# Gate and up products by a seven-product scheme over half of the k-tiles, with weight splits of 2048 elements

## The chip, the core and the metric

The kernel runs on one core of a Trainium2 chip. The metric is the device time of one execution in microseconds (us): 2843.92 us as the median of 3 runs (2843.08 to 2844.45).

## What is computed

Two decoder layers over 256 tokens of width 2048, all in f32: layer 0 mixes with latent attention (MLA), layer 1 with a gated delta rule (GDN). Each layer then has a SwiGLU feed-forward network (FFN) and a gated per-layer embedding (PLE).

```python
h = h + mixer(rms_norm(h, mixer_norm[i]), ...)
gate, up = jnp.split(rms_norm(h, ffn_norm[i]) @ w_gate_up[i], 2, axis=-1)   # 2048 x 11264
h = h + (jax.nn.silu(gate) * up) @ w_down[i]                                # 5632 x 2048
h = h + per_layer_embedding(h, p[i], ...)
```

## The kernel before

Every product with weights goes through `linear` (L216). The 256 tokens are two tiles of 128 (`T` = 2). An f32 operand is split in two fp32r parts, high and low, and a product takes three matmuls: high by high, high by low, low by high (L237 to L239). The transposed activations are split once and stay in SBUF; weights stream in. One load (L224, queue SP) brings four k-tiles by 512 columns, 1024 KB, into `raw`, of which there are three (`RB`). For each two k-tiles ScalarE casts the high part `wh` (L228) and VectorE subtracts it for the low part `wl` (L229), 1024 elements per partition each; five of each are in SBUF (`WB`, `WL`). Then 12 matmuls follow for the two k-tiles.

`ffn` (L471) walks 11 blocks of 512 columns in three parts (4, 4, 3). In a block, `linear` makes the gate (16 k-tiles, 96 matmuls) and then the up product (96 more). `evac_g` applies Silu on ScalarE, `evac_u` multiplies on VectorE into `md`; two k-tiles into the next block `make_xT` (L123) transposes `md` on TensorE (8 transposes) and splits it into `xh` (L137) and `xl` (L138). After a part, a down projection sums its blocks into the residual `h` (L251).

The program writes work in program order, with `tick` and `later` weaving side work in between; a scheduler then sets the order on each engine at compile time. Each engine runs its own list in order and waits on semaphores. A load on SP waits until the last reader of its buffer is through, and loads behind it wait with it. In the mixers the same `linear` streams the weights while attention or the delta rule runs between its k-tiles. `embed` (L499), the embedding's own projection, is woven into the last down projection.

Of the kernel before, what the change touches and what calls it, by code (L numbers as in the profile page):

```python
# [63 lines left out]
def trunk(ctx: ExitStack, tc: tile.TileContext, a: dict, out, plan=("mla", "ffn", "ple", "gdn", "ffn", "ple"), first=0):  # L64
# [151 lines left out]
    def linear(xs, W, kt, blocks, evac, row0=0, need=None):  # L216

        for bi, (c0, n) in enumerate(blocks):
            ps = [psmm.tile([P, 512], F32, tag="mm", name="mm") for _ in range(T)]
            for k4 in range(0, kt, 4):  # L220
                kn = min(4, kt - k4)
                raw = wp.tile([P, 4, 512], F32, tag="raw", name="raw", bufs=RB)
                r = row0 + k4 * P
                nc.sync.dma_start(out=raw[:, :kn, :n], in_=W[r:r + kn * P, c0:c0 + n].rearrange("(k p) n -> p k n", p=P))  # L224
                for k2 in range(0, kn, 2):
                    wh = wp.tile([P, 2, 512], F32R, tag="wh", name="wh", bufs=WB)
                    wl = wp.tile([P, 2, 512], F32R, tag="wl", name="wl", bufs=WL)
                    nc.scalar.copy(out=wh[:, :, :n], in_=raw[:, k2:k2 + 2, :n])  # L228
                    nc.vector.tensor_sub(out=wl[:, :, :n], in0=raw[:, k2:k2 + 2, :n], in1=wh[:, :, :n].bitcast(F32))  # L229
                    for kk in range(2):  # L230
                        k = k4 + k2 + kk
                        if need is not None:
                            need(k // 4)
                        until(lambda: len(xs) > k // 4)
                        for t in range(T):
                            xh, xl = part(xs, k, t)
                            mm(ps[t][:, :n], lhsT=xh, rhs=wh[:, kk, :n], start=(k == 0), stop=False)  # L237
                            mm(ps[t][:, :n], lhsT=xh, rhs=wl[:, kk, :n], start=False, stop=False)  # L238
                            mm(ps[t][:, :n], lhsT=xl, rhs=wh[:, kk, :n], start=False, stop=(k == kt - 1))  # L239
                        tick()  # L240
# [828 lines left out]
```

## Time and profile before

| what | us |
|---|---|
| runs, median of 3 | 2843.92 |
| the profiled execution, its own time | 2845.54 |
| its span, first to last instruction | 2843.8 |
| TensorE busy in the span | 2819.0 |
| VectorE busy | 1633.4 |
| ScalarE busy | 1370.4 |

The span is what the trace shows; 1.7 us of the execution's own time lie around it. In the trace PE is TensorE (PEld its weight loads), DVE is VectorE, ACT is ScalarE, POOL is GpSimd, SPq the queue that issues loads. Matmuls overlap in their pipeline, so the duration of one (0.39 us) is longer than the distance from one start to the next.

### The profile page before, as it was taken

The numbers are of one execution on the slowest core, as the hardware profiler recorded it, in microseconds if no ns is written. First come the engines' busy times: TensorE is split into PE (matmuls) and PEld (weight loads), VectorE is DVE, ScalarE is ACT, GpSimd is POOL, SyncE is SP. The second block draws the span as 40 slices with busy tenths as digits, with TensorE's granted clock in tenths as the row PEclk, the third lists the DMA queues.
The fourth block names the chain that finished last, engine by engine and source line by source line (L and its number), as shares of the span: only waits on it lengthen the run. The fifth ranks groups of instructions, "written<-read, shape, count | busy, mean of one in ns | idle before, by whom it ended". The sixth has DMA issues, their size and how long they took to land.

```text
span 2843.8 us, 34910 instructions
## 1 busy us (share of the span) xinstructions
PE 2819.0 (99%) x13873; PEld 2347.5 (83%) x13873; DVE 1633.4 (57%) x2064; ACT 1370.4 (48%) x1837; POOL 168.7 (6%) x254
## 2 busy tenths in 40 slices
PE   8999999999999999999999999999999999999999
PEld 8878888888888888888888888888888888888887
DVE  5675545545545656666674566657545545445654
ACT  6765444344444555655454444445444344444553
POOL 1330000000000000223100000000000000000000
PEclk9999999999999999999999999999999999999999
DMA  7435555555555555666777546455555555555554
GB/s 222 126 117 172 180 192 192 193 192 189 189 195 190 200 181 169 219 218 221 254 256 246 179 152 199 161 170 198 180 192 192 193 191 184 190 195 190 205 178 148
DMA packets 296454, 540.91 MB, mean 190 GB/s; under 512 B 34105, under 2 KB 55266, under 8 KB 296034
## 3 DMA queue, kind: packets, MB, share of 16 engines
q1 hardware_dynamic: 295858, 536.58, 57.0%
q8 instruction: 109, 1.79, 0.3%
q10 hardware_dynamic: 432, 2.10, 0.2%
q14 instruction: 55, 0.45, 0.0%
HBM read 517.63 MB, written 21.00 MB: 189 GB/s over the span
## 4 chain that ended last, share of the span: by engine, by line
PE 92%; DVE 3%; ACT 2%; DMA 1%; POOL 1%; issue 1%; SPq 0%; DVEq 0%; ACTq 0%; POOLq 0%
PE mm L237 28%; PE mm L239 28%; PE mm L238 28%; PE tr L132 2%; PE tr L814 1%; DVE wl L229 1%; PE tr L923 1%; PE tr L929 1%; DMA raw<-in_gdn_w_in 1%; ACT wh L228 1%; PE S L409 0%; PE tr L657 0%; PE S L408 0%; PE tr L681 0%; POOL E L734 0%
## 5 line engine op out<-in xcount | busy, mean ns | idle before, releaser
L229 DVE TENSOR_TENSOR wl<-raw,wh 128x1024 fp32r<-128x1024 f32 (+2 forms) x952 | 1149.7, 1211 | 1014.1 <-ACT wh L228 1013.4
L228 ACT CAST wh<-raw 128x1024 fp32r<-128x1024 f32 (+2 forms) x952 | 984.1, 1036 | 1243.6 <-PE mm L239 1202.3
L237 PE MATMUL mm<-wh,xh 128*128 128x512 f32 (+2 forms) x3776 | 1479.9, 392 | 3.0 <-ACT wh L228 3.0
L239 PE MATMUL mm<-wh,xl 128*128 128x512 f32 (+2 forms) x3776 | 1460.2, 387 | 0.0
L238 PE MATMUL mm<-wl,xh 128*128 128x512 f32 (+2 forms) x3776 | 1460.2, 387 | 0.0
L237 PEld LDWEIGHTS mm<-wh,xh 128*128 128x128 f32 x3776 | 712.0, 189 | 143.6 <-issue 5.3
L239 PEld LDWEIGHTS mm<-wh,xl 128*128 128x128 f32 x3776 | 711.4, 188 | 140.4 <-DVE xl L444 0.2
L238 PEld LDWEIGHTS mm<-wl,xh 128*128 128x128 f32 x3776 | 712.0, 189 | 133.1
L99 POOL TENSOR_TENSOR re<-re,neghalf 128x2 f32<-128x2 f32 x2 | 1.4, 696 | 1350.2 <-DVE re L521 1350.2
L251 DVE TENSOR_TENSOR h<-h,mm 128x512 f32<-128x512 f32 x88 | 56.6, 680 | 4.2 <-PE mm L239 4.2
L141 ACT ACTIVATE xh<-tr,ncol 128x256 fp32r<-128x256 f32 x104 | 46.9, 475 | 19.6 <-PE tr L132 13.2
L142 DVE SCALAR_TENSOR_TENSOR xl<-tr,ncol,xh 128x256 fp32r<-128x256 f32 x104 | 47.5, 482 | 5.3 <-ACT xh L141 3.3
L665 DVE SCALAR_TENSOR_TENSOR vT<-tr,cw,vT 128x255 f32<-128x255 f32 (+2 forms) x96 | 40.3, 473 | 2.0 <-ACT vT L244 1.5
L482 ACT ACTIVATE sg<-mm,rs 128x512 f32<-128x512 f32 x44 | 30.0, 690 | 20.8 <-PE mm L239 20.8
L976 POOL TENSOR_TENSOR r8o<-r8o,rq 128x8 f32<-128x8 f32 x8 | 5.2, 656 | 443.2 <-DVE r8o L972 443.2
L154 ACT ACTIVATE junk<-h 128x512 f32<-128x512 f32 x48 | 29.8, 623 | 3.5 <-DMA h<-in_x 2.6
L137 ACT CAST xh<-tr 128x512 fp32r<-128x512 f32 x44 | 23.8, 588 | 14.9 <-PE tr L132 14.9
L486 DVE SCALAR_TENSOR_TENSOR md<-mm,rs,sg 128x512 f32<-128x512 f32 x44 | 30.9, 743 | 0.0
L138 DVE TENSOR_TENSOR xl<-tr,xh 128x512 fp32r<-128x512 f32 x44 | 28.5, 685 | 2.1
L982 DVE SCALAR_TENSOR_TENSOR vb<-vb,r8o,zg 128x128 f32<-128x128 f32 x64 | 17.5, 346 | 19.9 <-POOL r8o L979 19.9
L244 ACT ACTIVATE xs<-mm,rs 128x512 f32<-128x512 f32 x32 | 21.5, 686 | 14.1 <-PE mm L239 14.0
L99 POOL TENSOR_TENSOR rs<-rs,neghalf 128x2 f32<-128x2 f32 x6 | 4.8, 806 | 387.1 <-DVE rs L174 387.1
(258 smaller groups left out, 1347.1 us busy)
## 6 DMA issues: line engine op xcount, KB each, us to landing
raw<-in_ffn_w_gate_up SPq DMA_DIRECT2D x176, 1024.0 KB, 5.0
raw<-in_gdn_w_in SPq DMA_DIRECT2D x92, 1024.0 KB, 5.4
raw<-in_ffn_w_down SPq DMA_DIRECT2D x88, 1024.0 KB, 5.1
raw<-in_ple_w_gate SPq DMA_DIRECT2D x32, 1024.0 KB, 5.1
raw<-in_gdn_w_out SPq DMA_DIRECT2D x32, 1024.0 KB, 5.1
raw<-in_mla_w_o SPq DMA_DIRECT2D x16, 1024.0 KB, 5.1
raw<-in_mla_w_ukv SPq DMA_DIRECT2D x8, 1024.0 KB, 5.2
raw<-in_mla_w_in SPq DMA_DIRECT2D x8, 768.0 KB, 4.8
```

What stands on the lines that cost most here:

```text
L132: nc.tensor.transpose(out=ps[:, o:o + P], in_=src(t)[:, kk * P:(kk + 1) * P], identity=ident)
L141: nc.scalar.activation(out=xh[:, s], in_=ps[:, c:c + n], func=AF.Copy, scale=w)
L142: nc.vector.scalar_tensor_tensor(out=xl[:, s], in0=ps[:, c:c + n], scalar=w, in1=xh[:, s].bitcast(F32), op0=ALU.mult, op1=ALU.subtract)
L228: nc.scalar.copy(out=wh[:, :, :n], in_=raw[:, k2:k2 + 2, :n])
L229: nc.vector.tensor_sub(out=wl[:, :, :n], in0=raw[:, k2:k2 + 2, :n], in1=wh[:, :, :n].bitcast(F32))
L237: mm(ps[t][:, :n], lhsT=xh, rhs=wh[:, kk, :n], start=(k == 0), stop=False)
L238: mm(ps[t][:, :n], lhsT=xh, rhs=wl[:, kk, :n], start=False, stop=False)
L239: mm(ps[t][:, :n], lhsT=xl, rhs=wh[:, kk, :n], start=False, stop=(k == kt - 1))
L251: nc.vector.tensor_add(out=h[bi][:, t, :], in0=h[bi][:, t, :], in1=ps[t])
L482: nc.scalar.activation(out=sg[:, t, :], in_=ps[t], func=AF.Silu, scale=nrm.rs[:, t:t + 1])
L486: nc.vector.scalar_tensor_tensor(out=md[:, t, :], in0=ps[t], scalar=nrm.rs[:, t:t + 1], in1=sg[:, t, :], op0=ALU.mult, op1=ALU.mult)
L665: nc.vector.scalar_tensor_tensor(out=acc[:, o + s:o + 256], in0=src[:, 0:256 - s], scalar=cw[:, jj * 64 + f:jj * 64 + f + 1], in1=acc[:, o ...
```

## The change

Of the 16 k-tiles of a gate/up block, the first eight now go through `seven`: token tile by k-half times k-half by gate or up is a product of 2x2 blocks, and it is formed from seven block products in place of eight. Call the weights of four k-tiles G0 to G3 (gate) and U0 to U3 (up); the code's b11, b12, b21, b22 are G0, U0, G1, U1, and r1, r2 are G2, U2 and then G3, U3. Four differences of weights are formed on VectorE (2048 elements per partition each): S1w = U0 - G0 and S2w = U1 - S1w, both in `tm`; S3w = U1 - U0 in U0's buffer; A22w = G1 - S2w in G1's buffer. Seven phases of 12 matmuls use G0, S1w, G1, S2w, U1, S3w and A22w, against sums of activations that `operands` forms once per FFN; eight phases of 12 do the other eight k-tiles as before. Between phases, copies of partial sums are made: ScalarE copies one PSUM bank to another (B from A) and two to SBUF (`m5`, `u2`); VectorE forms the fourth bank (D = A + m5) and adds u2 to `md`.

Weight splits take 2048 elements in one step (`step=4`) everywhere but in MLA's first projection (`step=2`). There are 3 tiles each of `raw`, `wh`, `wl`, and in an FFN 2, 1 and 1 more. An FFN has four parts (3, 3, 3, 2) instead of three. `embed` takes its small tiles from the pool `s4p`, with two in place of six for the rows of ple_norm.

```diff
+WBUFS = {"raw": 3, "wh": 3, "wl": 3}
+EXTRA = {"raw": 2, "wh": 1, "wl": 1}
-WB = 5
-WL = 5
-RB = 3
+    def wtile(kind, dt):
+        more = EXTRA[kind] if scope.get("extra") is not None else 0
+        i = turn[kind] % (WBUFS[kind] + more)
+        turn[kind] += 1
+        if i < WBUFS[kind]:
+            return wp.tile([P, 4, 512], dt, tag=kind, name=kind, bufs=WBUFS[kind])
+        return scope["extra"].tile([P, 4, 512], dt, tag=kind + "x", name=kind, bufs=more)
+    def wsplit(src, kn=4, n=512, step=4):
+        wh, wl = wtile("wh", F32R), wtile("wl", F32R)
+        for k in range(0, kn, step):
+            e = min(kn, k + step)
+            nc.scalar.copy(out=wh[:, k:e, :n], in_=src[:, k:e, :n])
+            nc.vector.tensor_sub(out=wl[:, k:e, :n], in0=src[:, k:e, :n], in1=wh[:, k:e, :n].bitcast(F32))
+        return wh, wl
...
+    def operands(self, b):
...
+            if b == 0:
+                one = p4("x11", F32R).rearrange("p (z k c) -> p z k c", z=2, k=4)
+                split(one[:, 0], one[:, 1], x4[:, :, 0, :])
...
+                split(xh, xl, xf)
+                nc.vector.tensor_add(out=f12[:, 0], in0=a21, in1=a22)
+                nc.vector.tensor_sub(out=f12[:, 1], in0=f12[:, 0], in1=a11)
+                nc.vector.tensor_sub(out=f34[:, 0], in0=a11, in1=a21)
+                nc.vector.tensor_sub(out=f34[:, 1], in0=a12, in1=f12[:, 1])
...
+    def phase(ps, x2, w2, start):
+            for kk in range(4):
+                xh, xl = x2(kk)
+                products(ps, (xh, xl), w2[0], w2[1], kk, 512, start and kk == 0, kk == 3, skip_group_check=True)
...
+        b11, b12 = wload(W, 0, c1), wload(W, 0, c2)
+        b21, b22 = wload(W, 512, c1), wload(W, 512, c2)
+        w2 = wsplit(b11)
+        phase(A, op("A11"), w2, True)
+        nc.vector.tensor_sub(out=tm, in0=b12, in1=b11)
+        w2 = wsplit(tm)
+        phase(C, op("S1"), w2, True)
+        nc.scalar.copy(out=B, in_=A)
+        nc.scalar.copy(out=m5, in_=C)
+        w2 = wsplit(b21)
+        phase(B, op("A12"), w2, False)
+        nc.vector.tensor_sub(out=tm, in0=b22, in1=tm)
+        w2 = wsplit(tm)
+        phase(A, op("S2"), w2, False)
+        nc.scalar.copy(out=u2, in_=A)
+        w2 = wsplit(b22)
+        phase(C, op("S4"), w2, False)
+        nc.vector.tensor_sub(out=b12, in0=b22, in1=b12)
+        w2 = wsplit(b12)
+        phase(A, op("S3"), w2, False)
+        nc.vector.tensor_add(out=D, in0=A, in1=m5)
+        r1, r2 = wload(W, 1024, c1), wload(W, 1024, c2)
+        q1 = wsplit(r1)
+        phase(B, std(2, 0), q1, False)
+        nc.vector.tensor_sub(out=b21, in0=b21, in1=tm)
+        w2 = wsplit(b21)
+        phase(A, op("A22"), w2, False)
+        q2 = wsplit(r2)
+        phase(A, std(2, 1), q1, False)
+        phase(C, std(2, 0), q2, False)
+        phase(D, std(2, 1), q2, False)
+        r1, r2 = wload(W, 1536, c1), wload(W, 1536, c2)
+        q1 = wsplit(r1)
+        phase(A, std(3, 1), q1, False)
+        phase(B, std(3, 0), q1, False)
+        evac(0, 1, A, None)
+        evac(0, 0, B, None)
+        q2 = wsplit(r2)
+        phase(C, std(3, 0), q2, False)
+        phase(D, std(3, 1), q2, False)
+        evac(1, 0, C, u2)
+        evac(1, 1, D, None)
...
-        parts = [range(0, 4), range(4, 8), range(8, NFF)]
+        parts = [range(0, 3), range(3, 6), range(6, 9), range(9, NFF)]
...
-                linear(nrm.x, wgu, 16, [(jb * 512, 512)], evac_g)
-                linear(nrm.x, wgu, 16, [(FF + jb * 512, 512)], evac_u)
+                seven(nrm, wgu, jb * 512, FF + jb * 512, evac_gu)
```

VectorE's list in the first FFN, from the end of one gate/up block into the next, before: L486 makes `md`, L138 its low part `xl`, and L229 the splits of the next block's weights.

```order
L486 SCALAR_TENSOR_TENSOR md_2953<-mm_3114,rs_2939,sg_2952 128x512
L486 SCALAR_TENSOR_TENSOR md_2953<-mm_3115,rs_2939,sg_2952 128x512
L229 TENSOR_TENSOR wl_3345<-raw_3342,wh_3344 128x1024
L229 TENSOR_TENSOR wl_3361<-raw_3342,wh_3360 128x1024
L138 TENSOR_TENSOR xl_3287<-tr_3288,xh_3286 128x512
L138 TENSOR_TENSOR xl_3287<-tr_3295,xh_3286 128x512
L229 TENSOR_TENSOR wl_3379<-raw_3376,wh_3378 128x1024
L229 TENSOR_TENSOR wl_3395<-raw_3376,wh_3394 128x1024
L229 TENSOR_TENSOR wl_3417<-raw_3414,wh_3416 128x1024
L229 TENSOR_TENSOR wl_3433<-raw_3414,wh_3432 128x1024
```

Of the change, at the same place: raw_3370, raw_3372, raw_3374, raw_3376 are G0, U0, G1, U1 of the next block, raw_3305 is U3 of the block that ends; L346 is S1w, L363 S3w, L356 S2w, L372 A22w.

```order
L346 TENSOR_TENSOR tm_3395<-raw_3372,raw_3370 128x2048
L110 TENSOR_TENSOR wl_3338<-raw_3305,wh_3337 128x2048
L110 TENSOR_TENSOR wl_3379<-raw_3370,wh_3378 128x2048
L363 TENSOR_TENSOR raw_3372<-raw_3376,raw_3372 128x2048
L110 TENSOR_TENSOR wl_3398<-tm_3395,wh_3397 128x2048
L356 TENSOR_TENSOR tm_3395<-raw_3376,tm_3395 128x2048
L110 TENSOR_TENSOR wl_3435<-raw_3374,wh_3434 128x2048
L634 TENSOR_TENSOR md_3091<-mm_3123,u2_3189 128x512
L372 TENSOR_TENSOR raw_3374<-raw_3374,tm_3395 128x2048
L636 SCALAR_TENSOR_TENSOR md_3091<-md_3091,rs_2798,sg_3090 128x512
L636 SCALAR_TENSOR_TENSOR md_3091<-mm_3224,rs_2798,sg_3090 128x512
L110 TENSOR_TENSOR wl_3452<-tm_3395,wh_3451 128x2048
```

The four differences now stand between the splits, and the step that makes `md` (L634, L636) stands among them. Next on VectorE:

```order
L161 TENSOR_TENSOR xl_3409<-tr_3410,xh_3408 128x512
L161 TENSOR_TENSOR xl_3409<-tr_3417,xh_3408 128x512
L110 TENSOR_TENSOR wl_3470<-raw_3376,wh_3469 128x2048
L110 TENSOR_TENSOR wl_3487<-raw_3372,wh_3486 128x2048
L110 TENSOR_TENSOR wl_3509<-raw_3504,wh_3508 128x2048
L110 TENSOR_TENSOR wl_3526<-raw_3374,wh_3525 128x2048
L110 TENSOR_TENSOR wl_3542<-raw_3506,wh_3541 128x2048
L367 TENSOR_TENSOR mm_3502<-mm_3382,m5_3432 128x512
```

After `xl` come the splits of U1, S3w, G2, A22w and U2 and then D (L367), which stood nowhere before; the eighth phase (A22w) writes the bank that D reads, and waits for it.

SP's list for the same blocks (raw_3226, raw_3228 and raw_3303 are G2, U2 and G3 of the block that ends):

```order
L101 DMA raw_3226<-in_ffn_w_gate_up 128x4x512
L101 DMA raw_3228<-in_ffn_w_gate_up 128x4x512
L101 DMA raw_3370<-in_ffn_w_gate_up 128x4x512
L101 DMA raw_3303<-in_ffn_w_gate_up 128x4x512
L101 DMA raw_3372<-in_ffn_w_gate_up 128x4x512
L101 DMA raw_3305<-in_ffn_w_gate_up 128x4x512
L101 DMA raw_3374<-in_ffn_w_gate_up 128x4x512
L101 DMA raw_3376<-in_ffn_w_gate_up 128x4x512
```

Four loads come one after the other here (G0, G3, U0, U3); they take the buffers of U1, U0, G2 and G1, and so follow the splits of U1, S3w, G2 and A22w on VectorE.

## Rows read from the trace of the kernel before

**Rows 1.** The page: span, and busy time of each engine.
```profile
span 2843.8 us, 34910 instructions
PE 2819.0 (99%) x13873; PEld 2347.5 (83%) x13873; DVE 1633.4 (57%) x2064; ACT 1370.4 (48%) x1837; POOL 168.7 (6%) x254
```
**Rows 2.** Busy time by stage: attention, first FFN, delta rule, second FFN; columns as headed.
```profile
core 0: us, PE busy (x) PEld busy (x) DVE busy (x) ACT busy (x) POOL busy (x), PEclk, DMA share, GB/s
0.00:275.00 275.00, 264.16 (x1362) 224.14 (x1363) 173.81 (x325) 177.77 (x423) 59.34 (x132) 1.00 0.49 157
275.00:1018.00 743.00, 742.78 (x3338) 615.84 (x3337) 388.28 (x374) 327.95 (x364) 4.95 (x6) 1.00 0.58 191
...
1110.00:2000.00 890.00, 883.21 (x5001) 737.57 (x5000) 577.23 (x877) 448.62 (x573) 101.64 (x112) 0.99 0.61 203
2000.00:2735.00 735.00, 734.78 (x3299) 609.13 (x3298) 384.24 (x368) 320.83 (x355) 1.39 (x2) 1.00 0.58 191
```
**Rows 3.** Timeline in an FFN block: start, duration, engine, line, operation [idle before, releaser].
```profile
640.03 0.39 PE L239 MATMUL mm<-wh,xl 128*128 128x512 f32 x1
...
640.26 0.39 PE L237 MATMUL mm<-wh,xh 128*128 128x512 f32 x1
...
640.46 1.05 ACT L228 CAST wh<-raw 128x1024 fp32r<-128x1024 f32 x1 [1.67 <-PE mm L239]
...
645.70 0.39 PE L237 MATMUL mm<-wh,xh 128*128 128x512 f32 x1
```
**Rows 4.** Timeline of VectorE over one gate/up block.
```profile
341.73 1.40 DVE L486 SCALAR_TENSOR_TENSOR md<-mm,rs,sg 128x512 f32<-128x512 f32 x2
343.31 1.23 DVE L229 TENSOR_TENSOR wl<-raw,wh 128x1024 fp32r<-128x1024 f32 x1 [0.18 <-ACT wh L228]
346.03 1.23 DVE L229 TENSOR_TENSOR wl<-raw,wh 128x1024 fp32r<-128x1024 f32 x1 [1.50 <-ACT wh L228]
347.36 1.29 DVE L138 TENSOR_TENSOR xl<-tr,xh 128x512 fp32r<-128x512 f32 x2
...
386.16 1.40 DVE L486 SCALAR_TENSOR_TENSOR md<-mm,rs,sg 128x512 f32<-128x512 f32 x2
```
**Rows 5.** One gate/up block, 387.0 to 431.5: all instructions, then VectorE's of L229.
```profile
387.00:431.50 44.50, 44.50 (x202) 36.96 (x201) 22.29 (x21) 19.30 (x21) 0.00 (x0) 1.00 0.57 189
...
387.00:431.50 44.50, 19.60 (x16) 1.00 0.57 189
```
**Rows 6.** Groups by line and form: count, busy us, mean ns, idle before.
```profile
L229 DVE TENSOR_TENSOR wl<-raw,wh 128x1024 fp32r<-128x1024 f32 x896 | 1100.4, 1231 | 979.4 <-ACT wh L228 978.8
L228 ACT CAST wh<-raw 128x1024 fp32r<-128x1024 f32 x896 | 941.4, 1052 | 1205.6 <-PE mm L239 1164.8 <-DMA raw<-in_gdn_w_in 16.4 <-issue 15.3
...
L251 DVE TENSOR_TENSOR h<-h,mm 128x512 f32<-128x512 f32 x88 | 56.6, 680 | 4.2 <-PE mm L239 4.2
...
L482 ACT ACTIVATE sg<-mm,rs 128x512 f32<-128x512 f32 x44 | 30.0, 690 | 20.8 <-PE mm L239 20.8
...
L138 DVE TENSOR_TENSOR xl<-tr,xh 128x512 fp32r<-128x512 f32 x44 | 28.5, 685 | 2.1
...
L228 ACT CAST wh<-raw 128x768 fp32r<-128x768 f32 x32 | 26.1, 834 | 12.4 <-PE mm L239 11.8 <-DMA raw<-in_mla_w_in 0.5
...
L137 ACT CAST xh<-tr 128x512 fp32r<-128x512 f32 x44 | 23.8, 588 | 14.9 <-PE tr L132 14.9
```
**Rows 7.** Timeline of VectorE in the delta-rule stage, three splits with no gap.
```profile
1238.29 3.49 DVE L229 TENSOR_TENSOR wl<-raw,wh 128x1024 fp32r<-128x1024 f32 x3
```
**Rows 8.** The page's DMA issues: count, KB each, median us from issue to landing.
```profile
raw<-in_ffn_w_gate_up SPq DMA_DIRECT2D x176, 1024.0 KB, 5.0
```
**Rows 9.** GB/s of 40 slices from 952 to 975 us.
```profile
GB/s 121 53 185 274 356 71 100 196 296 381 406 410 310 353 402 406 392 292 406 410 399 388 160 114 292 395 403 328 53 32 125 285 413 413 413 146 0 0 0 28
```
**Rows 10.** The page's chain that ended last, by engine.
```profile
PE 92%; DVE 3%; ACT 2%; DMA 1%; POOL 1%; issue 1%; SPq 0%; DVEq 0%; ACTq 0%; POOLq 0%
```
**Rows 11.** The same chain by line, from the view of the chain.
```profile
by line: PE mm L237 28.2%; PE mm L239 28.0%; PE mm L238 28.0%; PE tr L132 1.7%; PE tr L814 1.2%; DVE wl L229 1.0%; PE tr L923 1.0%; issue 0.8%; PE tr L929 0.7%; DMA raw<-in_gdn_w_in 0.7%; ACT wh L228 0.6%; PE S L409 0.4%; PE tr L657 0.4%; P
```
**Rows 12.** Pieces of that chain in the delta-rule stage: start, us, what.
```profile
1163.61 1.06 ACT wh L228
1164.69 1.24 DVE wl L229
...
1240.93 6.54 DMA raw<-in_gdn_w_in
...
1247.56 1.06 ACT wh L228
1248.65 1.22 DVE wl L229
1250.27 1.13 DVE wl L229
```

More of the change, by code (lines that the diff above doesn't have):

```diff
@@ L47 @@
 KY = 3
-P2 = {"mla": 14, "gdn": 8, "ffn": 6, "ple": 6}
+P2 = {"mla": 14, "gdn": 8, "ffn": 1, "ple": 6}
 def cody_waite():
@@ L177, in parts, with split @@
         def parts(self, b):
-            self.x.append(make_xT(lambda t: h[b][:, t, :], gain(self.wcol + 4 * b)))
+            if self.of7 and b < 2:
+                self.operands(b)
+            else:
+                self.x.append(make_xT(lambda t: h[b][:, t, :], gain(self.wcol + 4 * b)))
+        def operands(self, b):
+            xf = p4("xf")
+            w = gain(self.wcol + 4 * b)
+            for pair in range(2):
+                ps = trp()
+                for k2 in range(2):
+                    for t in range(T):
+                        kk = pair * 2 + k2
+                        nc.tensor.transpose(out=ps[:, k2 * 256 + t * P:k2 * 256 + (t + 1) * P],
+                                            in_=h[b][:, t, kk * P:(kk + 1) * P], identity=ident)
+                for k2 in range(2):
+                    scaled(xf[:, (pair * 2 + k2) * 256:(pair * 2 + k2 + 1) * 256], ps[:, k2 * 256:(k2 + 1) * 256],
+                           w[pair * 2 + k2])
+            x4 = xf.rearrange("p (k t c) -> p k t c", k=4, t=T)
+            def split(dh, dl, src):
+                nc.scalar.copy(out=dh, in_=src)
+                nc.vector.tensor_sub(out=dl, in0=src, in1=dh.bitcast(F32))
+            if b == 0:
+                one = p4("x11", F32R).rearrange("p (z k c) -> p z k c", z=2, k=4)
+                split(one[:, 0], one[:, 1], x4[:, :, 0, :])
+                self.one, self.xf = one, x4
+            else:
+                a11, a21 = self.xf[:, :, 0, :], self.xf[:, :, 1, :]
+                a12, a22 = x4[:, :, 0, :], x4[:, :, 1, :]
+                xh, xl = xpair()
+                split(xh, xl, xf)
+                f12, f34 = (p4(n).rearrange("p (z k c) -> p z k c", z=2, k=4) for n in ("f12", "f34"))
+                nc.vector.tensor_add(out=f12[:, 0], in0=a21, in1=a22)
+                nc.vector.tensor_sub(out=f12[:, 1], in0=f12[:, 0], in1=a11)
+                nc.vector.tensor_sub(out=f34[:, 0], in0=a11, in1=a21)
+                nc.vector.tensor_sub(out=f34[:, 1], in0=a12, in1=f12[:, 1])
+                self.two = []
+                for f in (f12, f34):
+                    dh, dl = xpair()
+                    split(dh, dl, f.rearrange("p z k c -> p (z k c)"))
+                    self.two.append([z.rearrange("p (z k c) -> p z k c", z=2, k=4) for z in (dh, dl)])
+                self.x += [None, (xh, xl)]
@@ L180, in block, with seven @@
+        def seven(self, name, kk):
+            until(lambda: hasattr(self, "one") if name == "A11" else hasattr(self, "two"))
+            if name == "A11":
+                return self.one[:, 0, kk], self.one[:, 1, kk]
+            if name in ("A12", "A22"):
+                return part(self.x, 4 + kk, int(name == "A22"))
+            i = int(name[1]) - 1
+            dh, dl = self.two[i // 2]
+            return dh[:, i % 2, kk], dl[:, i % 2, kk]
         def block(self, b, lag=0):
@@ L214, in until, with linear @@
             tick()
-    def linear(xs, W, kt, blocks, evac, row0=0, need=None):
+    def linear(xs, W, kt, blocks, evac, row0=0, need=None, step=4):
         for bi, (c0, n) in enumerate(blocks):
@@ L221, in linear @@
                 kn = min(4, kt - k4)
[L222 to L240, printed above, removed]
@@ L241, in linear @@
-            evac(bi, c0, n, ps)
+                raw = wload(W, row0 + k4 * P, c0, kn, n)
+                wh, wl = wsplit(raw, kn, n, step)
+                for kk in range(kn):
+                    k = k4 + kk
+                    if need is not None:
+                        need(k // 4)
+                    until(lambda: len(xs) > k // 4)
+                    for t in range(T):
+                        products(ps[t], part(xs, k, t), wh, wl, kk, n, k == 0, k == kt - 1)
+                    tick()
@@ L329, in mla @@
         linear(nrm.x, a["mla_w_in"][j], 16, [(0, 384), (384, 384), (768, 320)], evac_c,
-               need=lambda i: first_x(nrm, i))
+               need=lambda i: first_x(nrm, i), step=2)
         ssp = mc.tile([P, T], F32, name="ssp")
@@ L523, in embed @@
         for b in range(NB):
-            w = p2(name="pnw")
+            w = pw[:, 512:1024] if b % 2 else pw[:, 0:512]
             nc.sync.dma_start(out=w, in_=a["ple_norm"][i:i + 1, b * 512:(b + 1) * 512].partition_broadcast(P))
```

63 lines of the change are left out of this document (49 added, 14 removed).

## The prediction

> **What bounds the kernel now.** I read the page first. TensorE is busy for 2819.0 of 2843.8 us, VectorE for 57% and ScalarE for 48% [rows 1]; the chain that ended last is 92% TensorE, with VectorE 3%, ScalarE 2% and loads 1% [rows 10]. Busy time alone does not show a full engine, since matmuls overlap, so I then looked at the distance between starts. From 640.26 to 645.70 there are 24 matmuls: 5.44 us, or 0.2267 us each, with no gap [rows 3]. Then I checked whether a whole block keeps that pace. From one making of `md` to the next is 386.16 - 341.73 = 44.43 us [rows 4]. 192 matmuls at 0.2267 are 43.52, which leaves 0.91 us for the block's 8 transposes. So in an FFN TensorE's queue is the time, and a matmul taken away there is 0.2267 us gained as long as the other engines keep up. They have room now: in a block VectorE is busy 22.3 us and ScalarE 19.3 of 44.5 [rows 5], and each split on VectorE follows 1.5 us of waiting [rows 4]. The FFNs are 743 + 735 us of the span [rows 2]. In the mixers TensorE is less full (264 of 275 us with attention), and there splits and short operations stand on the chain.
>
> **Removed.** A block goes from 16 phases' worth of 12 matmuls to 15, and there are 2 x 11 blocks: 22 x 12 = 264 matmuls, x 0.2267 = **-59.8 us**. A block becomes 180 x 0.2267 + 0.91 = 41.7 us, if nothing else ends last.
>
> **Added on VectorE, per block.** Its price for 2048 elements is in no row. From 512 to 1024 elements a subtraction goes from 0.68 to 1.23 us [rows 6], so 2048 alone should take 1.23 + 2 x 0.55 = 2.3 us. Back to back they overlap: three of 1024 take 3.49 us, not 3 x 1.23 = 3.69 [rows 7], some 0.09 less from start to start, so I take 2.21. There are 11 splits and 4 differences, 15 x 2.21 = 33.2 us. D and the sum into `md` are 0.6 each, `md` is 1.40 and `xl` 1.29 [rows 4, 6]. Together 37 us of 41.7, where it was 22 of 44. VectorE is no longer loose: whether it keeps up is the question of this change, so I followed one block in the order given, with time 0 at the block's first phase and 2.72 us (12 x 0.2267) per phase.
>
> The first tight place is D. `xl` waits for the transposes, which stand after the second phase: 5.44 + 0.91 = 6.35. About 0.2 pass until TensorE's end is seen (a cast starts 0.43 after the start of the matmul it waits for, whose slot is 0.23 [rows 3]), ScalarE's `xh` takes 0.59 [rows 6], the last `xl` 0.69: 7.8. Then come five splits (U1, S3w, G2, A22w, U2), 11.05, and D, 0.68: 19.6. The eighth phase may write that bank after seven phases and the transposes, at 7 x 2.72 + 0.91 = 19.95. It fits by 0.35 us.
>
> The second is the loads. Four of the next block follow the splits of U1, S3w, G2 and A22w, 2.21 apart; the first is due at 7.8 + 2.2 = 10.0. One alone lands 5.0 us after issue [rows 8]. In bursts the queues reach 413 GB/s [rows 9], so 1.05 MB every 2.55 us, and the fourth lands at about 10.0 + 5.0 + 3 x 2.55 = 22.7. S1w of the next block may need it; VectorE is there at 21.8 (D, then the split of G3). Six operations later it meets the split of G1, which must wait until phase 13 frees a buffer (36.3 + 0.2), a Silu (0.69 [rows 6]) and a cast. A cast of 2048 is 1.05 + 4 x (1.05 - 0.83) = 1.93 [rows 6], so the split of G1 can start at 39.1, where VectorE has been waiting since 36.0. From there G1, `md`, A22w and S2w end at about 47.7, and the next block's `xl` is due at 48.8. It fits by 1.1 us. All 14 blocks that follow another block have this shape; the 8 that follow a down projection or open an FFN have no `md` in the way and start with three splits ahead.
>
> So I take TensorE as the bound and **+3 us** for the 0.35 us being missed now and then (14 x 0.2). The ends are 0 and a whole phase per such block, 14 x 2.72 = +38.
>
> ScalarE per block: 11 x 1.93 + 3 copies and 2 Silu at 0.69, 2 x 0.59 = 26 of 41.7 us, costed at nothing; the cover is TensorE, three splits ahead. The fourth part per FFN adds 8 additions to `h` (0.68 each) on VectorE under the down projection, where a split of 2.3 us covers 24 matmuls, 5.4 us: nothing. The operands are four additions of 0.68 and two more lows of 1.23 per FFN, some 5 us of VectorE spread under the last projection of the mixer: **+2 us** for both FFNs, ends 0 and 10. The two-tile row buffer in `embed` may hold VectorE for a few us, with three splits (16 us of TensorE) ahead: nothing.
>
> **Mixers.** Here a split step doubles. Where TensorE waits for a fresh load, a cast and a low part (1.06 + 1.24) become 1.93 + 2.30, 1.9 us more; six such pairs stand on the chain between 1163 and 1358, and in three of them the second half, 1.13, then falls away [rows 12]: 6 x 1.9 - 3 x 1.13 = +8. In attention there are a few single ones: +2. Buffers hold 12 k-tiles in place of 10, which helps a little. I take **+10**. The lower end is -10, about what TensorE idles in the attention stage (275 - 264 us [rows 2]); the upper end is all split pieces on the chain, 1.0% and 0.6% of the span or 45 us [rows 11], doubled: +45.
>
> **The sum.** -59.8 + 3 + 2 + 10 = -44.8 against the profiled execution's 2845.5 gives 2800.7. The median of the runs is 1.6 lower than that execution, so I say **2799**.
>
> [...] Rows 7 show VectorE starting the next of a row of operations 0.09 us before the last one's recorded end [rows 7]. [...]
>
> **Rivals.**
> 1. [...] Chance 0.18.
> 2. The mixers cost nothing, since deeper buffers balance the longer step: 2799 - 10 = 2789. For it: most splits there wait for buffers, not loads, since casts idle 1165 us for TensorE and 16 for loads [rows 6]. Chance 0.18.
> 3. Loads land one after the other, 5.0 us each, not overlapped. The fourth lands at 30.0; nine VectorE operations with `md`, `xl` and the split of U1 follow, and the loop closes at 45.4 us. The 14 blocks then lose 1.0 each against 44.43, the other 8 gain 2.72, the rest costs 12: 2848, no change. Against: 413 GB/s [rows 9]. Chance 0.07.
> 4. **Slower.** In the mixers each engine's list is served in order, and a step of 2.2 us holds up the short operations behind it, on VectorE and ScalarE alike. Those engines have 5% of the chain, 142 us [rows 10]; less 45 for splits [rows 11], that is some 170 short pieces of about 0.57. If each comes 0.2 later and all split pieces double, the mixers lose 45 + 34 = 79 and the time is 2843.9 - 59.8 + 5 + 79 = 2868. It decides from 61 us of loss. Against: TensorE is busy 883 of 890 us in the delta rule [rows 2], so most of those pieces have cover. Chance 0.10.
>
> That the change does not do what it says is excluded: the instruction lists hold 12 fewer matmuls in each block.
>
> **How the numbers follow.** The forecast has 0.47, rivals 1 to 4 have 0.18, 0.18, 0.07 and 0.10. 0.2% is 5.7 us, about the least that a measurement of this kernel can tell from no change. Faster: 0.47 + 0.18 + 0.18 = 0.83. Same: the third and a little of the fourth, 0.08. Slower: 0.09. The range runs from all of TensorE's gain, with a little gained in the mixers, 2782, to the forecast with VectorE's whole bound of 38, 2838; beyond it lie rivals 3 and 4.
>
> **What would show it.** In the profile after, 264 fewer matmuls; a block in the middle of a part between 41.7 and 42.3 us; VectorE near 37 us in it, D ending before the eighth phase; single 2048 splits of 2.3 us; FFN stages some 57 us shorter together, mixers some 10 longer. Wrong would be a block over 43 us, idle time of TensorE ended by L367 or by splits, or mixers longer by more than 30.

## The result

The changed kernel takes 2806.48 us (median of 4 runs, 2805.40 to 2807.84), beside 2843.50 for the kernel before on the same chip: ratio 0.987, 95% interval 0.9853 to 0.9887. That is 37 us faster, 7.5 us above the predicted 2799 and inside its range.

The last addition to `h` ends each stage, so its end in VectorE's timeline gives the length of the stage:

| stage | before, us | after, us | difference |
|---|---|---|---|
| attention | 298.58 | 300.12 | +1.5 |
| first FFN | 743.93 | 717.99 | -25.9 |
| first embedding | 92.45 | 92.14 | -0.3 |
| delta rule | 871.16 | 881.41 | +10.3 |
| second FFN | 743.86 | 720.50 | -23.4 |
| second embedding | 89.72 | 89.87 | +0.2 |

The mixers lost 11.8 us, where 10 were forecast. The FFNs gained 49.3, where 54.8 were (59.8 less 3 and 2). The first question is thus where 5 to 6 us of the FFNs' gain went, and the second what the mixers paid for.

The page after, its span and busy times, to be read beside [rows 1]:

```profile
span 2805.8 us, 33510 instructions
PE 2774.5 (99%) x13609; PEld 2300.1 (82%) x13609; DVE 1946.2 (69%) x1818; ACT 1443.5 (51%) x1517; POOL 161.6 (6%) x254
```

The 264 matmuls are gone (13873 - 13609), but TensorE's busy time fell by only 44.5 us. VectorE is 313 us busier with 246 fewer instructions.

One block inside a part of the second FFN, by busy time (columns as in [rows 2]), and VectorE's timeline up to its D (L367):

```profile
2056.00:2098.00 42.00, 42.00 (x190) 34.62 (x189) 37.41 (x22) 24.67 (x18) 0.00 (x0) 1.00 0.56 198
```

```profile
2232.44 1.29 DVE L161 TENSOR_TENSOR xl<-tr,xh 128x512 fp32r<-128x512 f32 x2
2233.64 6.68 DVE L110 TENSOR_TENSOR wl<-raw,wh 128x2048 fp32r<-128x2048 f32 x3
2241.09 4.58 DVE L110 TENSOR_TENSOR wl<-raw,wh 128x2048 fp32r<-128x2048 f32 x2 [0.77 <-ACT wh L109]
2245.59 0.69 DVE L367 TENSOR_TENSOR mm<-mm,m 128x512 f32<-128x512 f32 x1
...
2287.68 0.69 DVE L367 TENSOR_TENSOR mm<-mm,m 128x512 f32<-128x512 f32 x1
```

VectorE's 37.4 us are as forecast, and TensorE has no gap (42.00 of 42.00). From one D to the next are 42.09 us; the mean of 13 such distances, without the second FFN's first, is 42.05. The sum had 41.72. Since nothing waits, the matmuls themselves must be slower. TensorE's timeline in a down projection, first matmul of each triple (line L314):

```profile
456.86 0.39 PE L314 MATMUL mm<-wh,xh 128*128 128x512 f32 x1
...
457.54 0.39 PE L314 MATMUL mm<-wh,xh 128*128 128x512 f32 x1
...
458.22 0.40 PE L314 MATMUL mm<-wh,xh 128*128 128x512 f32 x1
...
463.73 0.40 PE L314 MATMUL mm<-wh,xh 128*128 128x512 f32 x1
...
465.12 0.40 PE L314 MATMUL mm<-wh,xh 128*128 128x512 f32 x1
...
465.82 0.39 PE L314 MATMUL mm<-wh,xh 128*128 128x512 f32 x1
...
469.90 0.39 PE L314 MATMUL mm<-wh,xh 128*128 128x512 f32 x1
```

A triple takes 0.68 us up to 458.22 and again from 465.82 (4.08 for six), but between them 11 triples take 7.60, 0.69 each. The slow stretch comes once in four splits of 2048, at a granted clock of 1.00. Before, the triples of [rows 3] and of four stretches of 40 to 60 us in the FFNs took 0.68 throughout. The mean over a stretch is 0.2280 us per matmul now; 0.0013 x 6072 FFN matmuls are 8 us. The FFN's own pool holds one more high and one more low split buffer (the fourth of each); in the compiled program these lie at bytes 209248 and 217440 of a partition, the three others of each below 94000.

One block stands out, at the opening of the second FFN: from D to D 44.88 us, with TensorE waiting for casts. VectorE's two D, and TensorE's two waits:

```profile
2009.18 0.69 DVE L367 TENSOR_TENSOR mm<-mm,m 128x512 f32<-128x512 f32 x1
2054.06 0.69 DVE L367 TENSOR_TENSOR mm<-mm,m 128x512 f32<-128x512 f32 x1
```

```profile
2011.31 0.50 PE L314 MATMUL mm<-wh,xh 128*128 128x512 f32 x1 [0.32 <-ACT wh L109]
2013.11 0.73 PE L314 MATMUL mm<-wh,xh 128*128 128x512 f32 x2 [1.30 <-ACT wh L109]
```

In the delta rule the doubled step is seen as short work behind a long split. Timeline of the delta rule, VectorE, ScalarE, TensorE:

```profile
1305.57 2.29 DVE L110 TENSOR_TENSOR wl<-raw,wh 128x2048 fp32r<-128x2048 f32 x1 [4.59 <-ACT wh L109]
1307.77 2.42 DVE L816 SCALAR_TENSOR_TENSOR kap<-tr,cw,kap 128x255 f32<-128x255 f32 x6
...
1311.57 1.06 ACT L821 ACTIVATE kap<-kap 128x1024 f32<-128x1024 f32 x1
1312.68 2.08 PE L868 MATMUL tr<-kap 128*128 128x128 f32 x8 [2.74 <-ACT kap L821]
```

Six small operations for `kap` stand behind a 2.29 us split; ScalarE's `kap` follows them, and TensorE has waited 2.74 us for that. The views of TensorE's waits in this stage (us in total, times, longest) name no load, cast or low part of weights, neither before (first row) nor after (the other two). Before, nothing waited for `kap`:

```profile
PE tr L681 <- ACT sq L676: 5.4, 4, 2.0
```
```profile
PE tr L868 <- ACT kap L821: 5.6, 2, 2.8
PE tr L832 <- ACT sq L827: 3.3, 1, 3.3
```

### The profile page after: what moved, and what is told of

The parts are those of the page before. It is cut to its first block, busy times and chain, and to the rows that moved or that the text cites. A ratio compares the mean times of both kernels' runs of the same rounds, so it can differ in the third digit from the quotient of the medians.

```text
span 2805.8 us, 33510 instructions
## 1 busy us (share of the span) xinstructions
PE 2774.5 (99%) x13609; PEld 2300.1 (82%) x13609; DVE 1946.2 (69%) x1818; ACT 1443.5 (51%) x1517; POOL 161.6 (6%) x254
## 4 chain that ended last, share of the span: by engine, by line
PE 50%; DVE 1%; ACT 1%; issue 1%; DMA 0%; POOL 0%; DVEq 0%; ACTq 0%
PE mm L314 15%; PE mm L316 15%; PE mm L315 15%; PE tr L965 1%; PE tr L1074 1%; PE tr L1080 1%; PE tr L155 1%; DVE wl L110 1%; ACT wh L109 0%; DMA raw<-in_ffn_w_gate_up 0%; PE tr L808 0%; PE tr L868 0%; PE tr L1055 0%; DVE vb L1133 0%; POOL r8o L122 0%
## 5 line engine op out<-in xcount | busy, mean ns | idle before, releaser
L110 DVE TENSOR_TENSOR wl<-raw,wh 128x2048 fp32r<-128x2048 f32 (+4 forms) x514 | 1120.7, 2191 | 546.6 <-ACT wh L109 545.6
L314 PE MATMUL mm<-wh,xh 128*128 128x512 f32 (+1 forms) x3600 | 1414.1, 393 | 5.2 <-ACT wh L109 5.1
L316 PE MATMUL mm<-wh,xl 128*128 128x512 f32 (+1 forms) x3600 | 1395.3, 388 | 0.0
L315 PE MATMUL mm<-wl,xh 128*128 128x512 f32 (+1 forms) x3600 | 1392.1, 387 | 0.9 <-DVE wl L110 0.9
L109 ACT CAST wh<-raw 128x2048 fp32r<-128x2048 f32 (+4 forms) x514 | 936.3, 1826 | 741.3 <-PE mm L316 588.6
L314 PEld LDWEIGHTS mm<-wh,xh 128*128 128x128 f32 x3600 | 678.4, 189 | 141.4 <-ACT wh L109 6.7
L109 ACT CAST wh<-tm 128x2048 fp32r<-128x2048 f32 x44 | 84.0, 1909 | 135.9 <-PE mm L316 115.0
L110 DVE TENSOR_TENSOR wl<-tm,wh 128x2048 fp32r<-128x2048 f32 x44 | 100.6, 2286 | 28.7 <-ACT wh L109 28.6
L346 DVE TENSOR_TENSOR tm<-raw 128x2048 f32<-128x2048 f32 x22 | 50.3, 2288 | 14.0 <-DMA raw<-in_ffn_w_gate_up 14.0
L363 DVE TENSOR_TENSOR raw<-raw 128x2048 f32<-128x2048 f32 x22 | 50.3, 2284 | 1.0 <-DMA raw<-in_ffn_w_gate_up 1.0
L356 DVE TENSOR_TENSOR tm<-raw,tm 128x2048 f32<-128x2048 f32 x22 | 50.4, 2292 | 0.7
L372 DVE TENSOR_TENSOR raw<-raw,tm 128x2048 f32<-128x2048 f32 x22 | 50.3, 2285 | 0.2
L314 PE MATMUL mm<-wh,x 128*128 128x512 f32 x88 | 34.5, 392 | 0.0
```

Source lines behind the costliest of these rows:

```text
L109: nc.scalar.copy(out=wh[:, k:e, :n], in_=src[:, k:e, :n])
L110: nc.vector.tensor_sub(out=wl[:, k:e, :n], in0=src[:, k:e, :n], in1=wh[:, k:e, :n].bitcast(F32))
L314: mm(ps[:, :n], lhsT=xh, rhs=wh[:, kk, :n], start=start, stop=False, **kw)
L315: mm(ps[:, :n], lhsT=xh, rhs=wl[:, kk, :n], start=False, stop=False, **kw)
L316: mm(ps[:, :n], lhsT=xl, rhs=wh[:, kk, :n], start=False, stop=stop, **kw)
L346: nc.vector.tensor_sub(out=tm, in0=b12, in1=b11)
```

## The experiments

The stage sums below come from the same ends of `h`; "pace" is the mean distance of matmuls in three FFN stretches.

**e1: the FFN's buffers exchanged.** Two unused tiles, allocated first, swap the places of the extra split and load buffers.

```diff
+            if s == "ffn":
+                for k, dt in (("wh", F32R), ("wl", F32R)):
+                    first = mc.tile([P, 4, 512], dt, tag=k + "x", name=k + "0", bufs=1)
+                    nc.vector.memset(first[:, 0, 0:1].bitcast(F32), 0.0)
```

> The changed kernel with the places of its FFN buffers in SBUF exchanged: the fourth high and fourth low split buffer, which lay at bytes 209248 and 217440 of a partition, come to 182624 and 190816, and the two extra load buffers go up instead. The instructions stay the same but for two one-column fills ahead of each FFN. Theory A: in the changed kernel the matmuls of the FFNs follow each other in 0.228 to 0.229 us on the mean, where they took 0.2267 before, because those that read (or stand beside a cast into) the two high-lying split buffers are slower; then the pace goes back to 0.2267, a block inside a part goes from 42.04 to about 41.7 us, and the time to about 2797. Theory B: the pace fell because VectorE and ScalarE are busier in long operations; then nothing changes, 0.228 and 2806.

2806.93 us, ratio 0.9862 (0.9848 to 0.9875); pace 0.2279 to 0.2281, FFNs as in the change (1438.6 us together). As put, A falls: 182624 is no better than 209248. B is not shown by that, since both places are far above the other six buffers. Its profiled execution, 2800.22, is 6.7 us under its median; the difference lies in the delta rule alone (below).

**e2: splits of 1024 outside the FFNs.**

```diff
-                wh, wl = wsplit(raw, kn, n, step)
+                wh, wl = wsplit(raw, kn, n, 4 if scope.get("extra") is not None else 2)
```

> The changed kernel with splits of 1024 elements in everything but the FFNs; buffers as in the change. Theory A: the 11.8 us that the mixers lost (MLA 1.5, delta rule 10.2) come from the doubled split step where TensorE waits for a fresh load; then both come back and the time is about 2795. Theory B: they come from the buffers (three of 2048 for high and low parts in place of five of 1024, freed a whole four k-tiles later); then the mixers stay where they are, 2806, or grow by the extra instructions.

2794.10 us, ratio 0.9824 (0.9811 to 0.9837), 12.4 under the change: theory A. Buffers are as in the change, so the step it is. Attention is back at 298.28, the delta rule at 868.92 us; the FFNs (1438.9) did not move. The delta rule's windows, before, the change, e1 and e2 (from end to end of the stage; span, then TensorE's busy time; the clock is the third number from the end):

```profile
1133.67:2004.84 871.17, 864.38 (x4910) 721.65 (x4909) 566.71 (x862) 438.37 (x554) 101.64 (x112) 0.99 0.62 205
```
```profile
1108.97:1990.39 881.42, 870.32 (x4915) 726.06 (x4914) 554.91 (x733) 419.41 (x428) 89.66 (x112) 0.98 0.61 204
```
```profile
1108.55:1982.98 874.43, 863.52 (x4917) 719.52 (x4916) 555.79 (x735) 419.77 (x428) 89.66 (x112) 0.99 0.62 206
```
```profile
1107.14:1976.02 868.88, 862.40 (x4910) 719.61 (x4909) 567.43 (x863) 432.44 (x557) 89.98 (x112) 0.99 0.62 207
```

TensorE idles 6.8, 11.1, 10.9 and 6.5 us. So some 4 of the 10.3 us that the delta rule lost are waits, and half the step takes them back. The other 6 are TensorE's busy time, 870.3 us instead of 864.4, at a granted clock of 0.98. The step alone does not set that: e1's profiled execution ran the same instructions of this stage at 0.99 and took 863.5. These clocks are means over two levels: of the stage's windows of 1 us, 850 of 871 show 1.00 and 13 show 0.50 before, 850 of 881 and 21 in the change. Here is a wait of TensorE in the change, the same one in e1, and for each the stretch near it at the lower level (0.50, at which the change's matmuls of weights start 0.43 us apart, 1.28 a triple from 1174.05 to 1175.33):

```profile
1166.63 1.65 PE L832 MATMUL tr<-ones,sq 128*128 128x1 f32 x7 [3.34 <-ACT sq L827]
1166.52 1.72 PE L832 MATMUL tr<-ones,sq 128*128 128x1 f32 x14 [3.14 <-ACT sq L827]
```
```profile
1165.65:1175.85 10.20, 9.22 (x30) 7.97 (x31) 2.37 (x2) 2.71 (x2) 5.19 (x4) 0.50 0.87 268
1168.60:1172.00 3.40, 3.40 (x9) 2.63 (x9) 2.27 (x2) 0.00 (x0) 3.25 (x1) 0.50 1.03 325
```

TensorE stood 3.34 us in the change and 3.14 in e1; the clock fell during that wait in the change, for 10.2 us, and 2 us after it in e1, for 3.4. Three of e1's four runs and all four of the change had a mean clock of 0.995 to 0.996, all five of e2 0.997. That the waits bring the clock down fits these runs, but was not tried by itself, and how long it stays down differs between executions of the same instructions.

**e3: the new splits and buffers with eight products.** `linear` makes gate and up as before; the activations' sums are left out.

```diff
-                seven(nrm, wgu, jb * 512, FF + jb * 512, evac_gu)
+                linear(nrm.x, wgu, 16, [(jb * 512, 512)],
+                       lambda bi, c0, n, ps: [evac_gu(0, t, ps[t], None) for t in range(T)])
+                linear(nrm.x, wgu, 16, [(FF + jb * 512, 512)],
+                       lambda bi, c0, n, ps: [evac_gu(1, t, ps[t], None) for t in range(T)])
...
```

> The changed kernel with its splits, buffers and parts, but gate and up by eight products as before: 264 matmuls and no differences, D or operands. Theory A (the high-lying split buffers slow the matmuls): the FFNs are slower than before too, pace about 0.2280, by some 2 x 3100 x 0.0013 = 8 us, and with the mixers' 11.8 the time is about 2864. Theory B (VectorE's and ScalarE's added work slows them): pace 0.2267, FFNs as before, time 2843.5 + 11.8 = 2855.

2863.13 us, ratio 1.0062 (1.0049 to 1.0074): A. Pace 0.2279 with VectorE at only half load, so B's cause (VectorE's added work) falls. The FFNs are 14.5 us longer than before: 8 by the pace, and 5.7 by a wait of TensorE that the change does not have. This row is from e3's view of waits:

```profile
PE tr L661 <- DMA pw<-in_p: 5.7, 2, 2.9
```

So the seven products alone are worth 57 us (2863.1 - 2806.5), and splits, buffers and parts without them cost 19 (2863.1 - 2844.5, the kernel before as measured beside it). The mixers keep the step of 2048 here. The delta rule takes 875.26 us, 4.1 more than before at a clock of 0.99, which agrees with some 4 us of waits. Attention takes 297.82, less than before, so its 1.5 us in the change cannot be put to the step alone.

**e4: seven products with splits of 1024 and the old five buffers.**

```diff
...
-        wh, wl = wtile("wh", F32R), wtile("wl", F32R)
-        for k in range(0, kn, step):
+        wh, wl = [], []
+        for k in range(0, kn, 2):
...
+            wh.append(wtile("wh", F32R))
+            wl.append(wtile("wl", F32R))
...
```

> The seven products with splits of 1024 elements and the five high and five low buffers of before; the two extra load buffers stay. Theory A: VectorE pays 22 x 1.2 for the splits of a block where it paid 11 x 2.25, and is some 39 to 40 of 41.7 us busy; D, with 0.35 us of room by the sum, comes 0.6 to 1 late, so a block inside a part takes 42.3 to 43 us; no split buffer lies high, so the pace is 0.2267; the mixers return to before, -11.8. Together about 2800. Rival: VectorE keeps up in the half steps as well, since each half can start as soon as its cast is there; then blocks of 41.7 and 2787. If VectorE cannot keep up at all, blocks over 44 us and a time over 2840.

2815.88 us, ratio 0.9899 (0.9886 to 0.9913). Pace 0.2267 and the mixers back, but blocks of 42.89 to 43.12: the upper end of A, 9 us slower than the change, so its 2800 was too low. The window of one block, and the view of waits:

```profile
2245.69:2288.73 43.04, 42.00 (x189) 34.48 (x188) 38.41 (x34) 26.42 (x30) 0.00 (x0) 1.00 0.55 195
```
```profile
PE mm L319 <- DVE wl L114: 15.9, 16, 1.1
```

VectorE is 38.4 us busy, so 4.6 are free, and still TensorE stands for 1.04 us a block. It waits for low parts, not for D. The edit takes away width and depth together: five buffers of two k-tiles hold 10 k-tiles, where four of four hold 16. Wide splits save only 1 us of VectorE a block (38.4 against 37.4), and e8 below, with wide splits and 12 k-tiles, loses time as well; what width is worth by itself was not tried.

**e5: all split buffers together, at the price of a load buffer.** On e2: `WBUFS` 2, 4, 4 and `EXTRA` 3, 0, 0.

> As e2_half (2794.1 us), but all four high and four low split buffers of the FFNs lie together with the others (bytes 36640 to 102176 of a partition), and the load buffers pay for it: two everywhere and three more in the FFNs. The exchange in e1_swap changed nothing in the pace (0.2281), but both places, 182624 and 209248, are far above the six other buffers. Theory A: matmuls that read a buffer up there, or stand beside a cast into it, are slow; then the pace of the FFNs is 0.2267, a block 41.7 to 41.8 us and the FFNs are some 8 us shorter together (6072 matmuls x 0.0013). Theory B: a rotation of four buffers, or casts of 2048, are slow wherever they lie; then the pace stays at 0.228. The mixers may lose a few us by having two load buffers in place of three. A: 2786 plus that; B: 2794 plus that.

2791.09 us, ratio 0.9809 (0.9795 to 0.9822). Pace 0.2267 in all three stretches, blocks 41.68 to 41.74 but for the second FFN's first (44.60), the FFNs 1425.1 together, 13.8 under e2; attention pays 6.8 and the delta rule 4.6, which the missing load buffer would explain. The 13.8 are some 6 more than the pace explains, which was not followed further. The places of the split buffers make the slow matmuls; a rotation of four buffers and casts of 2048 do not.

**e6: the same remainder.** As e2, with e1's tiles and a pad ahead of them.

```diff
+                pad = mc.tile([P, 368], F32, tag="pad", name="pad", bufs=1)
+                nc.vector.memset(pad[:, 0:1], 0.0)
```

> As e2_half, but the FFN's own high and low split buffer lie at 184096 and 192288, so that they leave the same remainder by 8192 (3872) as the six others; in e1_swap they lay at 182624 and 190816 (remainder 2400), in the change at 4448. If the remainder makes the slow matmuls: pace 0.2267 and about 2786. If the place does: pace 0.228 and 2794.

2787.34 us, ratio 0.9793 (0.9780 to 0.9807), pace 0.2267: the remainder, not the distance. It is the fastest version run, 19 us under the change by the medians. The same triples and two D from its timelines, for the rows of the change above:

```profile
441.52 0.39 PE L314 MATMUL mm<-wh,xh 128*128 128x512 f32 x1
...
442.88 0.39 PE L314 MATMUL mm<-wh,xh 128*128 128x512 f32 x1
```
```profile
2228.02 0.69 DVE L367 TENSOR_TENSOR mm<-mm,m 128x512 f32<-128x512 f32 x1
...
2269.72 0.69 DVE L367 TENSOR_TENSOR mm<-mm,m 128x512 f32<-128x512 f32 x1
```

Two triples take 1.36 us; from D to D are 41.70, the sum's 41.7. The FFNs take 1429.6 us together, 58.2 less than before.

**e7: only the high buffers together.** On e2: `WBUFS` 3, 4, 3 and `EXTRA` 2, 0, 1.

> As e2_half, but only the high split buffers lie together (four from 44832 on); of the low ones the fourth still lies high, at 217440. In the trace of e3_eight the slow stretch of 7.8 us in every 22 covers the matmuls that read the fourth buffers and the cast of ScalarE into the fourth high buffer after it, and not the subtraction into the fourth low buffer. If the high buffer alone makes it, the pace is 0.2267 and the time about 2786; if both do, somewhat under a third of the slow matmuls stay (pace 0.2271, 2788 to 2790).

2802.22 us, ratio 0.9845 (0.9831 to 0.9858): a miss on both counts. Pace 0.2280 to 0.2283, and attention 4.4 and the delta rule 5.2 us longer than in e2. TensorE's timeline at the end of a slow stretch and ScalarE's cast in it:

```profile
463.44 0.39 PE L314 MATMUL mm<-wh,xh 128*128 128x512 f32 x1
...
464.12 0.40 PE L314 MATMUL mm<-wh,xh 128*128 128x512 f32 x1
...
464.82 0.40 PE L314 MATMUL mm<-wh,xh 128*128 128x512 f32 x1
...
465.52 0.39 PE L314 MATMUL mm<-wh,xh 128*128 128x512 f32 x1
```
```profile
465.02 1.91 ACT L109 CAST wh<-raw 128x2048 fp32r<-128x2048 f32 x1 [3.65 <-PE mm L316]
```

The slow triples here take 0.70, so reading the low buffer alone costs as much as reading both. The cast starts when the reading of the fourth buffers is over; one slow triple follows (464.82 to 465.52). In the change three follow, up to 465.82, through the cast (463.93 to 465.84) into the high buffer that is off. That points to a second effect, matmuls slowed beside a write into such a buffer; it is not shown by itself.

**e8: three split buffers of each kind.** On e2: `EXTRA` 2, 0, 0.

> As e2_half, but three high and three low split buffers in the FFNs too, none high-lying. By the order of a block VectorE then works at most two splits ahead where it worked three: D, which follows five splits in a row, meets casts that wait for phases to end. Theory A: the pace is 0.2267 but blocks inside a part are longer than 43 us, because the casts of S3w and A22w wait for the third phase before them; time about 2800 to 2815. Rival: two splits ahead are enough, blocks of 41.8 us and 2787.

2807.59 us, ratio 0.9868 (0.9854 to 0.9881): the time of A, but not by its blocks of over 43. From D to D are 40.7 and 42.6 in turn and 109.7 over a down projection; it is the part that takes 2.6 us more than in e6, not each block. The view of waits:

```profile
PE mm L315 <- DVE wl L110: 12.6, 23, 1.1
```

So two splits ahead cost TensorE time, and three, in e6, cost it nothing inside a part.

**e9 and e10: which remainder.** As e6, with a pad of 64 bytes (`[P, 16]`) and of 1536 (`[P, 384]`).

> As e6_align (2787.3 us, pace 0.2267, the FFN's own split buffers at 184096 and 192288: remainder 3872 by 8192 and 32 by 128), but at 182688 and 190880, 64 bytes above the places of e1_swap: remainder 2464 by 8192, 32 by 128. If a fine remainder (by 128) makes the slow matmuls: pace 0.2267, 2787. If a coarse one (by some thousand bytes) does: pace 0.228 and 2794.

> As e6_align, but 64 bytes higher, at 184160 and 192352: remainder 3936 by 8192 and 96 by 128, as the 96 by 128 that the change (209248, 217440) and e1_swap (182624, 190816) have. By the fine remainder: pace 0.228 and 2794. By the coarse one: pace 0.2267 and 2787.

2795.91 (ratio 0.9829, 0.9816 to 0.9843), pace 0.2284; and 2796.22 (0.9829, 0.9816 to 0.9843), pace 0.2280. In e10, 64 bytes are enough to lose all that e6 gained, against the coarse remainder; in e9 a remainder of 32 by 128 does not help, against the fine one. Both theories fall as put. What all runs agree on: every fast buffer leaves 32 by 256 (as do the tiles of activations in the compiled program), every slow one 96 or 160. By 512, 1024, 2048 or 4096 they can be told apart just as well; which of these the chip goes by stays open.

**e11 and e12: 2.2 us more of VectorE, before D and after it.** As e6; the same value is made twice.

```diff
         w2 = wsplit(b12)
+        nc.vector.tensor_sub(out=w2[1], in0=b12, in1=w2[0].bitcast(F32))
```
```diff
         nc.vector.tensor_sub(out=tm, in0=b12, in1=b11)
+        nc.vector.tensor_sub(out=tm, in0=b12, in1=b11)
```

> As e6_align, but the low part of S3's weights is made twice, so VectorE does one more subtraction of 2048 in each block ahead of D; the rest of its order stays. In e6_align D ends at 2228.71, 0.36 us before its eighth phase may start (block start 2209.12 + 19.95 = 2229.07), and VectorE idles 0.68 between the added place and D. Theory A (a tight place decides): D ends 2.2 - 0.68 - 0.36 = 1.2 us too late, TensorE stops once per block, and blocks inside a part take 42.9 to 43.0 us; the time is 14 to 22 such stops higher, 2804 to 2813. Rival (only VectorE's sum counts): 37.4 + 2.2 = 39.6 of 41.7 us still fits, blocks of 41.7, 2787.

> As e6_align, but the first difference is made twice, so VectorE does the same 2.2 us more per block, this time behind D, where it idles some 2.7 us before the next block's xl. By the tight places: hidden, blocks of 41.7 to 41.9 us and 2787 to 2791. If the sum or the room ahead counts instead: blocks of 42.5 to 44 and 2800 or more.

e11: 2804.68 us (0.9860, 0.9847 to 0.9874); e12: 2792.89 (0.9817, 0.9804 to 0.9831). D to D, e11 and e12:

```profile
2244.39 0.69 DVE L368 TENSOR_TENSOR mm<-mm,m 128x512 f32<-128x512 f32 x1
...
2286.49 0.69 DVE L368 TENSOR_TENSOR mm<-mm,m 128x512 f32<-128x512 f32 x1
```
```profile
2233.66 0.69 DVE L368 TENSOR_TENSOR mm<-mm,m 128x512 f32<-128x512 f32 x1
...
2275.35 0.69 DVE L368 TENSOR_TENSOR mm<-mm,m 128x512 f32<-128x512 f32 x1
```

The same work costs 17 us ahead of D (42.07 to 42.31 per block) and 5.6 behind it, where blocks stay at 41.69 to 41.74 but for the first ones after an opening (up to 43.25). Part of both lies in the delta rule, which the edits do not touch: it takes 876.0 and 874.0 us, and 871.6 in e6. The FFNs, where the work was added, are 13.6 and 2.8 us longer than in e6 (1443.2 and 1432.4 against 1429.6). So a place counts and not only the sum.

The size was off: 0.4 to 0.6 us a block instead of 1.2, so that e11's time lies in A's range in part by luck. And it is not D that TensorE waits for. In e11's compiled program the scheduler put six of G2's matmuls into S3's phase and four of U2's ahead of A22's. Among these four TensorE stands for U2's low part, the last split ahead of D. Here are starts 0.39 and 0.33 us apart in place of 0.23, then the row of e11's view of waits and that of e6's:

```profile
2244.14 0.39 PE L314 MATMUL mm<-wh,xh 128*128 128x512 f32 x1
2244.53 0.50 PE L315 MATMUL mm<-wl,xh 128*128 128x512 f32 x1
2244.86 0.39 PE L316 MATMUL mm<-wh,xl 128*128 128x512 f32 x1
```
```profile
PE mm L315 <- DVE wl L110: 6.2, 10, 1.3
PE mm L315 <- DVE wl L110: 0.7, 2, 0.4
```

All but 0.7 of the 6.2 us fall into the first block of each FFN; the stops inside a part are too short for that view. A wait for D itself stands in none of these two views, and in e12's once, for 0.3 us. The tight place that the runs show is the row of splits just ahead of D. e12's 5.6 is above the 4 allowed: the first blocks were not in its sum, and the rest is the delta rule, as far as the profiled execution shows.

## Why the prediction was right, and where not

- **Removed: right.** 264 matmuls at 0.2267 are 59.8 us; in e6, where the pace holds, the FFNs are 58.2 shorter.
- **A block of 41.7: the step that failed.** "A block becomes 180 x 0.2267 + 0.91 = 41.7 us, if nothing else ends last": inside a part nothing did, but the 0.2267 of [rows 3] became 0.2280 by where two new buffers lie. Term mis-sized: 8 us by the pace; e6 stands 6.8 under e2 by the medians, 8.8 by the ratios. With the opening's 2.8 below, -59.8 + 8 + 2.8 is -49.0, against the 49.3 that the FFNs gained.
- **VectorE and D: right.** A split of 2048 takes 2.29 us alone, three take 6.68 (2.20 from start to start), and VectorE works 37.4 us. In e6, D ends at 2228.71, 19.59 us after its block's first phase (TensorE's first matmul with `x` starts at 2209.12); the sum said 19.6. Part of it is luck: the transposes come after one and a half phases, not two, and a wait of 0.68 for a cast takes that back. The +3 for D being missed was not spent: blocks inside a part take 41.7 in e5 and e6, and no wait of TensorE in the change is put down to D (L367). That left room in the sum for part of the 8 us above, which is luck too.
- **Operations of VectorE in a row: right.** The trace of the change has starts 2.20 us apart for operations of 2.28, as [rows 7] led one to expect; the prediction took 2.21.
- **FFN opening +2: too small** in the change, where the second FFN's first D to D alone is 2.8 over the rest, with TensorE waiting for casts. What sets it stays open: with half the step in the delta rule it is 42.99 in e2 and 42.55 in e6, but 44.60 in e5 and 44.88 in e7.
- **Mixers +10: right in size**, 11.8, and partly by luck. The step that failed is "Where TensorE waits for a fresh load, a cast and a low part": in the delta rule no wait of TensorE for these is seen, before or after. What grew is short work behind long splits, which is rival 4's mechanism: 5.6 us for `kap`, none before, and 2.1 less for `sq`. TensorE's idle time rose by 4.3 us there, where the term had 8. The other 6 of the 10.3 are TensorE's busy time at a lower granted clock (870.3 us at 0.98, 864.4 at 0.99 before), which had no term; e1's profiled execution did without them (863.5 at 0.99). Rival 4's price of 79 was far too high.
- **Rivals.** Loads one after another did not come true: blocks would have cost 1 us more than before. Mixers at no cost fell by e2, which had to halve the step to get them back.

## What to carry to other kernels

Where the sum over a busy engine's work says that a removed instruction is pure gain, check the pace of what remains as well as its count: here two new buffers slowed the FFNs' matmuls by 0.6% on the mean (0.2280 for 0.2267 us) with no wait to be seen. Splits of 2048 instead of 1024 saved 1 us of VectorE in a block of the FFNs (37.4 against 38.4), and lengthened waits where short work stood behind them (5.6 us for `kap` in the delta rule, none before); the step can be chosen per stage, and here that is 12 us. When an engine fills up, look for the place where it is due soonest: the same 2.2 us a block cost the FFNs 13.6 us ahead of it and 2.8 behind.

## What the runs showed of the hardware

Matmuls of fp32r, 128x512, follow each other every 0.2267 us in e5 and e6, where all split buffers leave the same remainder by 256 bytes, and every 0.230 to 0.233 in the change and in e7 while one is read that leaves another (triples of 0.69 and 0.70), at the same granted clock (1.00 in the change's slow stretch and in e6's blocks); 64 bytes decide it (pace 0.2267 in e6, 0.2280 in e10). Beside a cast of ScalarE into such a high buffer they seem to be slow too (three triples in the change, one in e7), which is not shown by itself. Whether the matter is a place by itself or that operands differ in it was not tried, and which remainder counts, from 256 to 4096, is open. The second surprise is the clock in the delta rule: the same instructions take 863.5 us of TensorE's time in e1 and 870.3 in the change, at a mean of 0.99 and 0.98, with 3.4 and 10.2 us at 0.50 near one and the same wait. At 0.50 matmuls in the change start 0.43 us apart, at 1.00 0.23.
